# A two-block network on one core: a joined gated-delta mixer, with its adaptive row products behind the inversion

## The chip, the cores and the metric

The kernel runs on one core of one Trainium2 chip. The metric is the device time of one execution in microseconds (us). A core has TensorE (matrix products into PSUM banks), VectorE and ScalarE (elementwise work, the latter with functions such as the exponential), GpSimd (POOL) and SyncE (SP), which issues most loads. The profile calls TensorE's products PE and its weight loads PEld, VectorE DVE and ScalarE ACT.

## The reference, cut to what matters

Everything is fp32: a sequence of 256 tokens of width 1024 beside a context of 256 tokens. The first block is adaptive norm, a mixer, and a convolutional gated feed-forward net (FFN). Two further layers of other mixers and MLPs follow; the change hardly touches them.

```
mod = silu(c) @ w_ada + b_ada                    # shifts, scales and gates of the norms
q, k, v = silu(dwconv1d(h @ w_in, conv))         # 4 heads of 128; q and k then l2-normed
beta = sigmoid(ab); g = -exp(a_log) * softplus(ab + dt_bias)
gc    = cumsum(g in a chunk)
decay = where(lower, exp(gc[i] - gc[j]), 0)
a_mat = where(strict, (beta * k) @ k.T * decay, 0)
t_inv = inverse(eye + a_mat)                     # one per head, chunk, direction, sequence
for chunk: v_new = u - w @ S;  o = q_dec @ S + attn @ v_new;  S = S * exp(g_last) + k_dec.T @ v_new
y = concat(fourier(u), rmsnorm(o) * silu(z)) @ w_out
ffn: (silu(conv3x3(gate)) * val) @ w_down
```

The rule runs over the context first and then over the sequence, forward and backward.

## The kernel before, in words

Products in fp32 are mostly done in a split form: ScalarE copies a weight tile to a rounded high part (`whi`, L155) and VectorE subtracts it for the low part (`wlo`, L156). Three products then stand for one: high by high, high by low, low by high. Some products are plain fp32 (`cmn`, `tmn`). SP loads weights as tiles of 1 MB (`raw`, L161).

The mixer (`_block1_mix`, about 38 to 260 us) works on both sequences, s = 1 (context) and s = 0. For each it makes the gates (`gates1`, `gdn_scalars`, softplus and roots with few columns), projects and convolves k, turns it and multiplies it with itself (`kk`), and makes the decay masks (`decay`, L947: `gr - gc` plus the mask on VectorE, then one exponential). The scaled masks `Mall` (L785) hold 32 matrices of 128x128. `invert` turns their diagonal blocks of 32x32 with four transposes (L1029), solves all of them at once in 31 pairs of steps (L1039, L1041), and turns the results back (L1045). `merge` joins the 32-blocks on TensorE (y, z, zt), and `chain_step` runs the rule over four steps of chunks. Fourier products and gate products (`pu`) fill in between.

The adaptive rows (`ada_dot`) are a list of small pieces that `fill_step` issues at marked points: GpSimd's queue loads 512 KB into one of two tiles `nar` (L255), and one VectorE instruction (L259) takes its dot products. 10 of the first block's 24 stand before the inversion's end.

`project_out` (w_out) multiplies by its first half of channels, yields, and then by the second half, whose inputs come out of the rule. `begin` prepares the first two weight units of the FFN early and multiplies the first tokens (`part`, L496) as soon as they are normed. Engines run their instructions in the order in which a scheduler put them by priorities (`AHEAD`, `URGENT`) and dependences; a tile in a pool waits for the reader of the one whose place it takes. In the FFN each of 11 hidden tiles takes two weight units, a 3x3 convolution in 8 VectorE steps per half (L1290), and a product with w_down (L1274), two hidden tiles later.

Of the kernel before, what the change touches and what calls it, by code (L numbers as in the profile page):

```python
# [66 lines left out]
class Program:  # L67
# [67 lines left out]
    def softplus(self, out, in_, n):  # L135

        nc = self.nc
        T = lambda s: self.sm.tile([128, 16], F32, name=self.nm(s), tag=s, bufs=2)[:, :n]
# [25 lines left out]
    def units(self, src, count, nb, early=0):  # L164


        for u in range(count):
# [209 lines left out]
    def finish(self, banks, G, mod=None, between=None):  # L377
# [27 lines left out]
        with self.tc.high_priority(offset=URGENT):  # L405
            if mod is None:
                for t in range(2):
                    gain(t, 0)
                    gain(t, 1)
                    y[t][0](0)  # L410
                    y[t][0](1)
# [31 lines left out]

            gain(0, 0)
            gain(0, 1)
            y[0][0](0)
            y[0][0](1)
# [99 lines left out]
    def block1_mix(self):  # L547
        nc, tc = self.nc, self.tc
        self.yT = None
        with ExitStack() as ctx:  # L550
            self.work = self.pool(ctx, "work1", 2)
            self.nw1, self.ng2, self.nt2 = 6, 6, 1
# [72 lines left out]
    def conv_start(self, ps, i, out):  # L625

        nc = self.nc
        w = self.cwh
        x = self.W1("cvx")
# [3 lines left out]
        def rest():  # L633
            nc.vector.scalar_tensor_tensor(out=out[:, 1:], in0=x[:, :255], scalar=w[:, 3 * i:3 * i + 1], in1=out[:, 1:],
                                           op0=ALU.mult, op1=ALU.add)
            nc.vector.scalar_tensor_tensor(out=out[:, :255], in0=x[:, 1:], scalar=w[:, 3 * i + 2:3 * i + 3], in1=out[:, :255],
# [6 lines left out]
    def _block1_mix(self, g):  # L643
# [52 lines left out]
        pow_ = self.pow  # L696
        mods = next(mods)
        self.halves()
        del self.scratch
        for s in seqs:  # L700
            for k in range(8):
# [3 lines left out]
                else:  # L705
                    last = nc.vector.tensor_scalar(out=hT[s][k], in0=hT[s][k], scalar1=A[:, k:k + 1], scalar2=sh[:, k:k + 1], op0=ALU.mult, op1=ALU.add)
        wab = T([128, 8, 16], "wab", "wab")
        nc.sync.dma_start(wab, a["w_ab"])
        gates = {s: self.gates1(wab, hT[s], g, s) for s in seqs}
        for s in seqs:  # L710
            next(gates[s])

# [9 lines left out]
        def unit(u):  # L722
            return self.load(a["w_in"][u]).rearrange("p (k n) -> p k n", k=8)

        def split_unit(u, places):
            w = self.load(a["w_in"][u])
            with ExitStack() as ctx:
                if u >= 4:
                    ctx.enter_context(tc.issue_after(conv.ins))
                for i in range(2):  # L730
                    self.split(places[i], places[2 + i], w[:, i * 1024:(i + 1) * 1024])
# [7 lines left out]

        E, early = {}, deque((1, t, d) for t in range(2) for d in range(2))  # L740
        kT = {s: T([128, 4, 256], "kT", f"kT{s}") for s in seqs}
        kn = {s: T([128, 2, 4, 128], "kn", f"kn{s}") for s in seqs}
        ssq = {s: self.const.tile([128, 2, 4], F32, name=f"ssq{s}") for s in seqs}
        for u in range(2):
            w = split_unit(u, room("Zall") if u == 0 else room("atT0", "ut", "atT1", "sz"))
            for s in seqs:
                for m in range(2):
                    h = 2 * u + m
                    ps = self.PB("pk")
                    self.cm(ps, w, hp[s], m)  # L750
                    conv = self.conv_silu(ps, h, kT[s][:, h])
                    if (u, s, m) == (0, 1, 1):
                        self.hold = conv
                        gate = {s: next(gates[s]) for s in seqs}
                        scalars = {s: self.gdn_scalars(gate[s], ssq[s], g, s) for s in seqs}
                        gc = {s: next(scalars[s]) for s in seqs}
                    pt = self.pst.tile([128, 2, 128], F32, name=self.nm("tk"), tag="pst")
                    for t in range(2):
                        nc.tensor.transpose(pt[:, t], in_=kT[s][:, h, t * 128:(t + 1) * 128], identity=self.ident)
                    nc.scalar.activation(kn[s][:, :, h], pt, AF.Copy)  # L760
                    for t in range(2):
                        j = self.sm.tile([128, 128], F32, name=self.nm("j"), tag="j", bufs=2)
                        nc.scalar.activation(j, kn[s][:, t, h], AF.Square, accum_out=ssq[s][:, t, h:h + 1])
                    if u == 1 and early:
                        i = early.popleft()
                        E[i] = self.decay(gate[1][1], gc[1], i[2], i[1], None)
        sc = {s: next(scalars[s]) for s in seqs}
# [4 lines left out]
        Mall = T([128, 2, 2, 2, 4, 128], "Mall", "Mall")  # L772
        kd = {}
        for s in seqs:
            for t in range(2):
# [4 lines left out]
                for d in range(2):  # L780
                    if (s, t, d) not in E:
                        E[s, t, d] = self.decay(gate[s][1], gc[s], d, t, atT[t][:, d] if s == 0 else None)
                    e = E[s, t, d]
                    for h in range(4):
                        nc.vector.scalar_tensor_tensor(out=Mall[:, d, s, t, h], in0=kk[:, h], scalar=sc[s]["m"][:, d, t, h:h + 1],  # L785
                                                       in1=e[:, h], op0=ALU.mult, op1=ALU.mult)

        for s, ts in ((1, 0), (1, 1), (0, 0)):
            z = T([128, 2, 4, 128], "kd", "kd", bufs=3)
            for d in range(2):  # L790
                t = ts if s == 1 else d
                kd[d, s, t] = z[:, d]
                for h in range(4):
                    with tc.issue_after(roots.ins):
                        nc.gpsimd.tensor_scalar(out=z[:, d, h], in0=kn[s][:, t, h], scalar1=sc[s]["kd"][:, d, t, h:h + 1], scalar2=None, op0=ALU.mult)
# [1063 lines left out]
```

## Time and profile before

| | |
|---|---|
| median of 3 runs | 1671.67 us (1668.91 to 1674.85) |
| profiled execution | 1665.61 us, span 1663.8 us, granted clock 0.985 |
| PE busy | 1583.1 us (95%) |
| PEld busy | 1385.8 us (83%) |
| DVE busy | 1246.9 us (75%) |
| ACT busy | 866.7 us (52%) |
| POOL busy | 67.9 us (4%) |

The shares are means over stages with different limits. The mixer takes up to about 270 us, the first FFN about 300 to 505, the two layers the rest. A busy PE is not one at its peak: matmuls are pipelined, and the granted clock is a mean of two levels.

### The profile page before, as it was taken

The page shows a single profiled execution, that of the slowest core. Times are in us where ns is not written, and L with a number is a line of the kernel's source. Part 1 is how long each engine was busy: PE and PEld are TensorE (multiplying, and loading weights), DVE is VectorE, ACT ScalarE, POOL GpSimd, SP SyncE. Part 2 cuts the span into 40 slices and gives each one's busy share as a digit, 9 for nine tenths or more (in the row PEclk, how much of TensorE's full clock was granted, in tenths as well). Part 3 has the DMA queues.
Part 4 walks back from the last instruction along what each step waited for, and adds up shares of the span by engine and source line. Part 5 has one row for each costly group of instructions (what it writes and reads, how often), then busy time and mean ns, then how long its engine had stood idle before and what let it go on. Part 6 is the DMA issues. An engine that isn't in the chain of part 4 may idle for free.

```text
span 1663.8 us, 24724 instructions
## 1 busy us (share of the span) xinstructions
PE 1583.1 (95%) x9584; PEld 1385.8 (83%) x9584; DVE 1246.9 (75%) x2237; ACT 866.7 (52%) x1452; POOL 67.9 (4%) x103
## 2 busy tenths in 40 slices
PE   7969997999978999999999999999999999999998
PEld 2867986889967998888888899889988888879997
DVE  5898664899996794797768767777948877786554
ACT  4734453555445664655446544466646455564443
POOL 1150100000000000000000000000000000000000
PEclk9989999999988999999999999999999999999999
DMA  9332514456773554465665758746444656656552
GB/s 381 127 116 93 172 66 152 165 211 230 259 287 145 204 206 174 161 227 213 228 230 188 271 210 286 283 178 222 178 176 159 250 192 227 240 202 253 180 191 86
DMA packets 51669, 333.59 MB, mean 200 GB/s; under 512 B 6112, under 2 KB 6496, under 8 KB 14688
## 3 DMA queue, kind: packets, MB, share of 16 engines
q1 hardware_dynamic: 47808, 318.38, 52.5%
q0 software_dynamic: 3744, 13.63, 2.4%
q8 instruction: 75, 1.23, 0.3%
q14 instruction: 42, 0.34, 0.1%
HBM read 330.94 MB, written 1.05 MB: 200 GB/s over the span
## 4 chain that ended last, share of the span: by engine, by line
PE 75%; DVE 10%; ACT 5%; issue 5%; DMA 4%; POOL 1%; DVEq 0%; SPq 0%; POOLq 0%; ACTq 0%
PE pj L208 25%; PE pj L227 22%; PE bk L1274 11%; PE bk L227 4%; DVE wlo L156 2%; PE pj L496 2%; ACT whi L155 2%; DMA raw<-adaT 2%; PE pu L218 1%; DVE gac L1290 1%; DVE raw L259 1%; DMA raw<-w_down 1%; ACT xn L369 1%; DMA x<-x 1%; PE pk L208 1%
## 5 line engine op out<-in xcount | busy, mean ns | idle before, releaser
L156 DVE TENSOR_TENSOR wlo<-raw,whi 128x1024 fp32r<-128x1024 f32 x438 | 521.3, 1222 | 256.9 <-ACT whi L155 255.3
L155 ACT ACTIVATE whi<-raw 128x1024 fp32r<-128x1024 f32 x438 | 446.9, 1055 | 420.5 <-PE pj L208 177.4
L208 PE MATMUL pj<-hT,whi 128*128 128x256 f32 x2816 | 371.1, 284 | 5.5 <-ACT gac L1232 3.2
L208 PEld LDWEIGHTS pj<-hT,whi 128*128 128x128 f32 x2816 | 354.4, 192 | 10.6 <-ACT gac L1232 3.6
L1274 PE MATMUL bk<-whi,hid 128*128 128x512 f32 x688 | 187.7, 394 | 18.1 <-ACT hid L155 18.1
L208 PE MATMUL pj<-hT,wlo 128*128 128x256 f32 x1408 | 198.9, 284 | 0.0
L208 PEld LDWEIGHTS pj<-hT,wlo 128*128 128x128 f32 x1408 | 182.5, 193 | 0.4 <-issue 0.4
L227 PE MATMUL pj<-whi,hT 128*128 128x512 f32 x704 | 177.4, 394 | 0.6 <-ACT rgx L1693 0.6
L1274 PEld LDWEIGHTS bk<-whi,hid 128*128 128x128 f32 x688 | 127.3, 190 | 44.9 <-ACT hid L155 20.0
L227 PEld LDWEIGHTS pj<-whi,hT 128*128 128x128 f32 x704 | 130.9, 188 | 27.9 <-ACT rgx L1693 1.4
L259 DVE CUSTOM_DVE_ANT_0 raw<-raw,crow 128x1024 f32<-128x1024 f32 x104 | 124.9, 1221 | 10.5 <-DMA raw<-adaT 10.3
L1274 PE MATMUL bk<-wlo,hid 128*128 128x512 f32 x344 | 106.5, 391 | 0.0
L227 PE MATMUL pj<-wlo,hT 128*128 128x512 f32 x352 | 94.2, 389 | 0.0
L227 PEld LDWEIGHTS pj<-wlo,hT 128*128 128x128 f32 x352 | 66.1, 188 | 13.9
L1274 PEld LDWEIGHTS bk<-wlo,hid 128*128 128x128 f32 x344 | 65.0, 189 | 14.0
L1290 DVE SCALAR_TENSOR_TENSOR gac<-gin,cols,gac 128x189 f32<-128x189 f32 (+2 forms) x176 | 66.4, 430 | 1.8 <-ACT gac L1232 1.7
L496 PE MATMUL pj<-whi,hT 128*128 128x512 f32 x160 | 54.8, 413 | 2.0 <-POOL hT L441 1.1
L373 POOL TENSOR_TENSOR ss<-ss,nhalf 128x1 f32<-128x1 f32 x22 | 12.2, 554 | 811.2 <-DVE ss L372 811.2
L496 PEld LDWEIGHTS pj<-whi,hT 128*128 128x128 f32 x160 | 30.4, 194 | 12.1 <-ACT hT L432 2.9
L155 ACT ACTIVATE hid<-r 128x512 fp32r<-128x512 f32 x32 | 20.2, 630 | 36.5 <-DVE r L1326 36.4
L259 DVE CUSTOM_DVE_ANT_0 nar<-nar,crow 128x1024 f32<-128x1024 f32 x24 | 29.3, 1222 | 8.9 <-DMA nar<-adaT 8.8
L432 ACT ACTIVATE hT<-tp,sh,A 128x128 fp32r<-128x128 f32 x80 | 30.2, 460 | 10.9 <-PE tp L425 7.5
(429 smaller groups left out, 2200.3 us busy)
## 6 DMA issues: line engine op xcount, KB each, us to landing
raw<-w_in SPq DMA_DIRECT2D x98, 1024.0 KB, 4.9
raw<-mlp_w SPq DMA_DIRECT2D x64, 1024.0 KB, 4.9
raw<-adaT SPq DMA_DIRECT2D x52, 1024.0 KB, 4.9
raw<-w_up SPq DMA_DIRECT2D x22, 1024.0 KB, 4.9
nar<-adaT POOLq DMA_DIRECT2D x24, 512.0 KB, 4.3
raw<-w_out SPq DMA_DIRECT2D x12, 1024.0 KB, 4.8
raw<-w_down SPq DMA_DIRECT2D x11, 1024.0 KB, 5.0
raw<-lru_w_o SPq DMA_DIRECT2D x8, 1024.0 KB, 4.8
```

The lines of the kernel that those rows point to most:

```text
L155: self.nc.scalar.activation(hi, v, AF.Copy)
L156: self.nc.vector.tensor_tensor(out=lo, in0=v, in1=hi.bitcast(F32), op=ALU.subtract)
L208: self.nc.tensor.matmul(ps, lhsT=ww[k][:, m * 128:(m + 1) * 128], rhs=xx[k], start=(i == 0 and k == 0), stop=(i == 2 and k == 7))
L218: self.nc.tensor.matmul(ps, lhsT=x[k][:, t * 128:(t + 1) * 128], rhs=w[:, k, :], start=(k == 0), stop=(k == 7))
L227: self.last_product = self.nc.tensor.matmul(ps, lhsT=xx[k0 + k][:, t * 128:(t + 1) * 128], rhs=ww[k], start=(k0 == 0 and i == 0 and k == 0 ...
L259: nc.vector.tensor_tensor_reduce(out=r, in0=r, in1=self.crow[vec], scale=0.5, scalar=0.0, op0=ALU.mult, op1=ALU.add, accum_out=out[:, k:k ...
L369: self.queue("a", lambda: nc.scalar.activation(junk[:, i * 512:(i + 1) * 512], parts[i], AF.Square, scale=1.0 / 32, accum_out=ss[:, i:i + 1]))
L373: self.queue("g", lambda: nc.gpsimd.tensor_tensor(out=ss[:, 3:4], in0=ss[:, 2:3], in1=self.nhalf, op=ALU.pow))
L432: q("a", lambda: nc.scalar.activation(H[0][k][:, tk(t)], ps[t, g][:, j], AF.Identity, scale=A[:, k:k + 1], bias=sh[:, k:k + 1]))
L496: self.nc.tensor.matmul(self.early[t], lhsT=H[lo][k][:, tk], rhs=ww[k % 4], start=(lo == j == i == 0), stop=(lo == 1 and j == 7))
L1274: self.last_product = self.nc.tensor.matmul(banks[t][h], lhsT=xx[:, k, t * 128:(t + 1) * 128], rhs=ww[k][:, h * 512:(h + 1) * 512], start= ...
L1290: self.nc.vector.scalar_tensor_tensor(out=acc[:, r, c], in0=gin[:, ri, ci], scalar=w, in1=acc[:, r, c], op0=ALU.mult, op1=ALU.add)
```

## The change

1. Gates and scalars are made for both sequences in one set, with softplus over 32 columns and one root over 16. Sums of decays are turned into rows (`gcrows`), in a high and a low part. `decay` spreads a row on TensorE: a product that puts the mask into the bank, and four that add the row; ScalarE's exponential takes the other sum as its bias. The scale of v moves into kd and into `ro`, so that `chain_step` copies v plainly.
2. k and v of both sequences are convolved in pairs, 512 columns in a tile. The first unit of k is plain fp32.
3. ScalarE copies the diagonal blocks into `invD`, with 128 rows, so that one transpose goes each way; eight copies put the result into `Zall`.
4. `fill_step` is no longer called among v's convolutions. It is called in the chain, where it now waits for the inversion, the roots and the copies, and once in each gate unit. q's convolutions are finished behind the first merge.
5. Four units of w_out take places that are free in the mixer; the last of the four is loaded into the pool `more`.
6. w_down's units are loaded straight into `whi` and `wlo` places as two halves of 512 KB, and the products are plain fp32 with an unsplit hidden tile.
7. `finish` squares before it multiplies by the gain; in the MLPs the hidden tiles from 14 on have a high priority.

The core of the diff:

```
     for h in range(4):
-        nc.tensor.matmul(gr[:, h], lhsT=gg[:, d, t, h:h + 1].to_broadcast([128, 128]),
-                         rhs=self.U if d == 0 else self.L, start=True, stop=True)
...
+            nc.tensor.matmul(gr, lhsT=self.mask[:, 0], rhs=self.mask[:, mask:mask + 1].to_broadcast([128, 4, 128]), start=True, stop=False)
             for h in range(4):
-                nc.vector.scalar_tensor_tensor(out=e[:, h], in0=gr[:, h], scalar=gc[:, d, t, h:h + 1], in1=mask,
-                                               op0=ALU.subtract, op1=ALU.add if sign > 0 else ALU.subtract)
-            nc.scalar.activation(e, e, AF.Exp, scale=float(sign))
+                i = 16 * d + 4 * h + 2 * s + t
+                nc.tensor.matmul(gr[:, h], lhsT=self.choose[:, i:i + 1].to_broadcast([64, 128]), rhs=self.gcrows, start=False, stop=h == 3)
+            for h in range(4):
+                nc.scalar.activation(e[:, h], gr[:, h], AF.Exp, scale=float(sign), bias=gc[sign][:, d, h, s, t:t + 1])
...
+                for b in range(4):
+                    q = slice(32 * b, 32 * b + 32)
+                    nc.scalar.activation(D[q, :, s, t], Mall[q, :, s, t, :, q], AF.Copy)
...
-        for b in range(4):
-            q = slice(32 * b, 32 * b + 32)
-            nc.vector.transpose(B[q].rearrange("m j i -> m i j"), Mf[q, :, q].rearrange("j m i -> j i m"))
+        nc.vector.transpose(B.rearrange("m j i -> m i j"), Df.rearrange("j m i -> j i m"))
...
+                    for s in seqs:
+                        self.cmn(ps[:, s], w, hT[s], m)
...
-                    if m == 0:
-                        with tc.issue_after(last.ins), tc.issue_after(pow_.ins), tc.issue_after(self.hold.ins):
-                            self.fill_step()
...
-                with tc.issue_after(self.turned_back.ins):
+                with tc.issue_after(self.turned_back.ins), tc.issue_after(roots.ins), tc.issue_after(self.z_copied.ins):
                     self.fill_step()
...
-        self.wout = self.project_out("w_out", yT, EARLY)
+        self.wout = self.project_out("w_out", yT, 4)
...
+            if plain:
+                with self.tc.high_priority(offset=AHEAD):
+                    tiles = [self.hl.tile([128, 1024], F32R, name=self.nm(tag), tag=tag, bufs=self.nhl).bitcast(F32) for tag in ("whi", "wlo")]
+                    for h, z in enumerate(tiles):
+                        self.nc.sync.dma_start(z, src(u)[:, h * 1024:(h + 1) * 1024])
+                yield Weights(tiles, nb(u)), None
+                continue
...
-        p = [(whi, hid[:, 0]), (whi, hid[:, 1]), (wlo, hid[:, 0])]
+        p = [(whi, hid[:, 0]), (whi, hid[:, 1]), (wlo, hid[:, 0])] if wlo else [(whi, hid)]
```

VectorE's row before, at the start of the inversion (`invB` the turned blocks, `nar` with `gc` an adaptive dot, `qT` and `vT` convolutions):

```order
L636 SCALAR_TENSOR_TENSOR qT_1038<-cvx_1138,cwh,qT_1038 128x255
L1029 STREAM_TRANSPOSE invB<-Mall_906 32x32x32 x4
L259 ISA nar_1452,gc_1265<-nar_1452,crow_1266 128x1024
L259 ISA gc_1265 128x1
L1039 TENSOR_TENSOR invt<-invB,invX 128x31
L634 SCALAR_TENSOR_TENSOR vT_1277<-cvx_1278,cwh,vT_1277 128x255
L1041 TENSOR_TENSOR invX<-invX,invt 128x31
L639 SCALAR_TENSOR_TENSOR qT_1038<-cvx_1138,qT_1038 128x256
```

and the same place now:

```order
L645 SCALAR_TENSOR_TENSOR qT_897<-cvx_962,cwh,qT_897 128x255
L1069 STREAM_TRANSPOSE invB<-invD_739 128x32x32
L648 SCALAR_TENSOR_TENSOR qT_897<-cvx_934,qT_897 128x256
L648 SCALAR_TENSOR_TENSOR qT_897<-cvx_962,qT_897 128x256
L1079 TENSOR_TENSOR invt_1035<-invB,invX 128x31
L643 SCALAR_TENSOR_TENSOR qT_897<-cvx_997,cwh,qT_897 128x255
L1081 TENSOR_TENSOR invX<-invX,invt_1035 128x31
L643 SCALAR_TENSOR_TENSOR qT_897<-cvx_1025,cwh,qT_897 128x255
```

One transpose over 128 rows stands for four over 32, and no adaptive dot is left there; the first one now stands in VectorE's row among the merge's and the chain's steps (`Zall`, `zc` parts of the merge, `pqs` and `qs` of q's root):

```order
L246 SCALAR_TENSOR_TENSOR crow_1424<-nar_1426,crow_1424 128x1024
L648 SCALAR_TENSOR_TENSOR vT_1249<-cvx_1250,vT_1249 128x512
L1198 TENSOR_SCALAR Zall<-z_1299 32x4x32 x2
L267 ISA nar_1429,gc_1423<-nar_1429,crow_1424 128x1024
L267 ISA gc_1423 128x1
L1198 TENSOR_SCALAR zc_1282<-z_1313 32x4x32 x2
L267 ISA nar_1430,gc_1423<-nar_1430,crow_1424 128x1024
L267 ISA gc_1423 128x1
L1198 TENSOR_SCALAR Zall<-z_1341 64x4x64
```

All 24 dots follow in this manner, one or two between the steps.

ScalarE's row before, at the end of the mixer (`raw_2567` and `raw_2577` the FFN's first two units, `raw_2499` and `raw_2509` the second half of w_out, `yv` the rule's outputs):

```order
L155 ACTIVATE whi_2569<-raw_2567 128x1024
L155 ACTIVATE whi_2573<-raw_2567 128x1024
L155 ACTIVATE yT_2367<-yv_2459 128x256
L155 ACTIVATE yT_2367<-yv_2466 128x256
L155 ACTIVATE yT_2367<-yv_2473 128x256
L155 ACTIVATE whi_2579<-raw_2577 128x1024
L155 ACTIVATE whi_2583<-raw_2577 128x1024
L155 ACTIVATE yT_2367<-yv_2480 128x256
L155 ACTIVATE whi_2501<-raw_2499 128x1024
L155 ACTIVATE whi_2505<-raw_2499 128x1024
L155 ACTIVATE whi_2511<-raw_2509 128x1024
```

and now (`raw_2299` and `raw_2309` the second half of w_out, `raw_2367` the FFN's first unit):

```order
L155 ACTIVATE whi_2301<-raw_2299 128x1024
L155 ACTIVATE whi_2305<-raw_2299 128x1024
L155 ACTIVATE yT_2163<-yv_2259 128x256
L155 ACTIVATE yT_2163<-yv_2266 128x256
L155 ACTIVATE yT_2163<-yv_2273 128x256
L155 ACTIVATE whi_2311<-raw_2309 128x1024
L155 ACTIVATE whi_2315<-raw_2309 128x1024
L155 ACTIVATE yT_2163<-yv_2280 128x256
L377 ACTIVATE xn_2389,ss_2391<-bk_2182 128x512
L377 ACTIVATE xn_2389,ss_2391<-bk_2183 128x512
L155 ACTIVATE whi_2369<-raw_2367 128x1024
```

The second half of w_out is split ahead of the FFN's units. The load of `raw_2309` into the pool `more`, whose place lies over tiles of the mixer, waits for the last product of the first half.

## Rows read from the trace of the kernel before

**Rows 1.** Totals of the page: busy us (share), instructions.

```profile
PE 1583.1 (95%) x9584; PEld 1385.8 (83%) x9584; DVE 1246.9 (75%) x2237; ACT 866.7 (52%) x1452; POOL 67.9 (4%) x103
```

**Rows 2.** Windows: busy us of PE, PEld, DVE, ACT, POOL; clock; DMA share; GB/s.

```profile
38.00:163.00 125.00, 106.67 (x666) 92.60 (x666) 115.74 (x339) 64.22 (x179) 30.07 (x40) 0.95 0.34 118
121.00:163.00 42.00, 37.54 (x182) 30.78 (x182) 39.70 (x108) 21.02 (x63) 2.32 (x2) 0.96 0.26 89
163.00:270.00 107.00, 105.90 (x770) 93.00 (x770) 57.38 (x153) 43.43 (x124) 8.93 (x15) 1.00 0.35 119
270.00:307.30 37.30, 27.18 (x121) 21.19 (x122) 30.12 (x54) 25.13 (x50) 3.51 (x5) 0.91 0.37 131
345.00:487.00 142.00, 142.00 (x984) 133.22 (x983) 137.97 (x245) 74.12 (x98) 0.00 (x0) 0.99 0.67 246
487.00:508.00 21.00, 7.98 (x25) 5.89 (x24) 14.26 (x26) 5.77 (x11) 0.56 (x1) 0.67 0.50 175
```

**Rows 3.** Chain of waits, 70 to 125 us: start, length, what.

```profile
78.01 2.58 POOL rs L133
...
100.00 4.54 DVE wk L156 x4
...
110.06 2.09 DVE invB L1029
...
120.71 39.69 issue
```

**Rows 4.** Groups on DVE, 38 to 163 us: count; busy us, mean ns; idle before.

```profile
L259 DVE CUSTOM_DVE_ANT_0 nar<-nar,crow 128x1024 f32<-128x1024 f32 x10 | 12.2, 1222 | 0.0
L1041 DVE TENSOR_TENSOR invX<-invX,invt 128x31 f32<-128x31 f32 (+15 forms) x31 | 10.5, 339 | 0.4
...
L1029 DVE STREAM_TRANSPOSE invB<-Mall 32x1024 f32<-32x1024 f32 x4 | 8.6, 2150 | 0.0
L947 DVE SCALAR_TENSOR_TENSOR E<-gr,gc,cst 128x128 f32<-128x128 f32 x24 | 7.2, 342 | 0.3 <-PE gr L942 0.3
...
L947 DVE SCALAR_TENSOR_TENSOR atT<-gr,gc,cst 128x128 f32<-128x128 f32 x16 | 4.5, 341 | 0.0
L634 DVE SCALAR_TENSOR_TENSOR kT<-cvx,cwh,kT 128x255 f32<-128x255 f32 x8 | 3.9, 482 | 0.6 <-ACT kT L631 0.6
```

**Rows 5.** Chain of waits, 163 to 310 us.

```profile
246.36 13.81 PE pu L218 x64
...
269.63 4.76 DMA raw<-w_up
274.50 1.07 ACT whi L155
...
279.57 12.58 PE bk L227 x48
```

**Rows 6.** What PE waited for: us in total, times, longest.

```profile
PE bk L1274 <- ACT hid L155: 18.1, 5, 12.7
PE bk L227 <- ACT whi L155: 8.4, 1, 8.4
```

**Rows 7.** Products of 512 columns: two rows of the chain, one of PE's timeline.

```profile
233.94 1.73 PE f L1163 x4
...
355.62 5.47 PE bk L1274 x24
...
221.56 1.98 PE L1163 MATMUL f<-dft,ut 128*128 128x512 f32 x4
```

**Rows 8.** Adaptive dots: landing of their loads, waits for them, first and last issue.

```profile
  DVE nar L259: 8.8, 6
...
DMA to landing us min/median/max: 3.9/4.4/13.1
...
162.07 0.69 POOL L255 DMA_DIRECT2D nar<-adaT  x1
...
206.83 0.53 POOL L255 DMA_DIRECT2D nar<-adaT  x1 [2.83 <-DVE A L259]
```

More of the change, by code (lines that the diff above doesn't have):

```diff
@@ L162, in load, with units @@
         return r
-    def units(self, src, count, nb, early=0):
+    def units(self, src, count, nb, early=0, plain=False):
         for u in range(count):
@@ L407, in finish @@
                 for t in range(2):
[L408 to L411, printed above, removed]
+                    for h in range(2):
+                        y[t][0](h)
+                        gain(t, h)
                     y[t][1]()
@@ L720, in _block1_mix @@
         hp = {s: (Blocks(parts[s][:2]), Blocks(parts[s][2:])) for s in seqs}
-        def unit(u):
-            return self.load(a["w_in"][u]).rearrange("p (k n) -> p k n", k=8)
         def split_unit(u, places):
             w = self.load(a["w_in"][u])
[L727 to L731, printed above, removed]
+            for i in range(2):
+                self.split(places[i], places[2 + i], w[:, i * 1024:(i + 1) * 1024])
             return Weights(places[:2], 256), Weights(places[2:], 256)
@@ L738, in room, with unit @@
             return [T([128, 1024], "wk", t, F32R) for t in tags]
+        def unit(u):
+            return self.load(a["w_in"][u]).rearrange("p (k n) -> p k n", k=8)
         E, early = {}, deque((1, t, d) for t in range(2) for d in range(2))
-        kT = {s: T([128, 4, 256], "kT", f"kT{s}") for s in seqs}
-        kn = {s: T([128, 2, 4, 128], "kn", f"kn{s}") for s in seqs}
-        ssq = {s: self.const.tile([128, 2, 4], F32, name=f"ssq{s}") for s in seqs}
-        for u in range(2):
[L745 to L757, printed above, removed]
@@ new lines, in _block1_mix @@
+        kTs = T([128, 2, 4, 256], "kT", "kT")
+        kT = [kTs[:, s] for s in range(2)]
+        kns = T([128, 2, 2, 4, 128], "kn", "kn")
+        kn = [kns[:, s] for s in range(2)]
+        ssq = self.const.tile([128, 4, 2, 2], F32, name="ssq")
+        for u in range(2):
+            w = split_unit(u, room("Zall")) if u else unit(u)
+            for m in range(2):
+                h = 2 * u + m
+                ps = self.PB("pk", (128, 2, 256))
+                for s in seqs:
+                    if u:
+                        self.cm(ps[:, s], w, hp[s], m)
+                    else:
+                        self.cmn(ps[:, s], w, hT[s], m)
+                self.conv_silu(ps, h, kTs[:, :, h])
+                if h == 0:
+                    gate = next(gates)
+                    scalars = self.gdn_scalars(gate, ssq, g)
+                    gc = next(scalars)
+                pt = self.pst.tile([128, 2, 2, 128], F32, name=self.nm("tk"), tag="pst")
+                for s in seqs:
@@ L764, in _block1_mix @@
[L764 to L767, printed above, removed]
+                        nc.scalar.activation(j, kn[s][:, t, h], AF.Square, accum_out=ssq[:, h, s, t:t + 1])
+                if u == 1:
+                    for i in (early.popleft(), early.popleft()):
+                        E[i] = self.decay(gc, 1, i[2], i[1], None)
+        sc = next(scalars)
@@ new lines, in gates1 @@
+        ab = {}
+        for s in (1, 0):
+            ps = (self.pst if s else self.psd).tile([16, 256], F32, name=self.nm("ab"), tag="pst" if s else "psd")
+            for k in range(8):
+                nc.tensor.matmul(ps, lhsT=wab[:, k, :], rhs=hT[s][k], start=(k == 0), stop=(k == 7))
+            ab[s] = self.work.tile([16, 256], F32, name=self.nm("abs"), tag="w1", bufs=self.nw1)
+            nc.scalar.activation(ab[s], ps, AF.Copy)
+        yield
+        ps = self.pst.tile([128, 2, 2, 16], F32, name="abt", tag="pst")
@@ new lines, in gates1 @@
+        for s in (1, 0):
+            for t in range(2):
+                nc.tensor.transpose(ps[:, s, t], in_=ab[s][:, t * 128:(t + 1) * 128], identity=self.ident[0:16, 0:16])
+        pc = ps.rearrange("p s t c -> p c (s t)")
+        beta = g.tile([128, 2, 4, 2, 2], F32, name="beta")
+        gg = g.tile([128, 2, 4, 2, 2], F32, name="gg")
+        by = lambda z: z.rearrange("p d h s t -> p (d h) (s t)")
+        fl = lambda z: z.rearrange("p d h s t -> p (d h s t)")
+        xx = self.sm.tile([128, 8, 4], F32, name="xx", tag="xx", bufs=1)
```

274 lines of the change are left out of this document (148 added, 126 removed).

## The prediction

> **What bounds the kernel now.** I read the page's totals first. TensorE is busy 95% of the span [rows 1], so a stage gains only where it idles or loses matmuls. The windows show where that is: from 38 to 163 us, where the decay masks and the 32x32 inversions are made, it has 106.7 of 125 us, 18.3 us idle, while VectorE has 115.7; from 163 to 270, the chain over the chunks, TensorE has 105.9 of 107; from 270 to 307.3 it idles 10.1; from 345 to 487 it is full, VectorE having 138; the end of the first FFN (487 to 508) has 8 us of matmuls in 21 at a granted clock of 0.67, a mean of its two levels (1.2 and 2.4 GHz) after VectorE's splits left TensorE idle [rows 2]. After 508 the change hardly moves an instruction.
>
> The chain of waits says what holds the first stretch: the root on GpSimd, the scaled masks on VectorE, then block transposes and 39.7 us of "issue", short steps with no named wait [rows 3]. VectorE's groups give the durations [rows 4]. The chain from 246 to 292 and the list of TensorE's waits give the next two places [rows 5, 6]. The span is 1663.8 us and the profiled execution 1665.61; the median of the runs shown, 1671.67, is 6.1 us above it. Differences are worked out in the profile and put on the median.
>
> **Up to the inversion's end.** VectorE's work in 38 to 163 falls by parts:
> - The adaptive dots leave: 10 x 1.222 = 12.2 [rows 4], and one row of weights made once, about as long as one: 13.4 us.
> - The block transposes: 8 of 2.15 us on 32 partitions [rows 4] become 2 on all 128 with the same 1024 elements per partition: 17.2 to 4.3, 12.9 us less. If duration went with all elements, each would take 8.6 and nothing would be saved; I take the lower end, since all rows of VectorE here go by the elements per partition: 0.34 us for 128, 1.22 for 1024, on 128 partitions.
> - L947's 40 additions go: 7.2 + 4.5 = 11.7 us [rows 4]. TensorE spreads the rows instead: for each of 10 masks a 128x512 product (0.228 us by 5.47/24 [rows 7]) and four of 128 columns, against 32 fp32 products of 128 columns (7 us at 0.22, half of the 256-column pitch below). At 0.06 us per narrow product, a quarter of 0.228, it is 4.7 us, 2.3 less; at fp32's 0.22 it is 11.1, 4.1 more. I take 0, between them: this stretch has idle TensorE time for either.
> - Convolutions of pairs: 8 fewer groups of three calls save the fixed part of 24 calls. From 0.48 us at 255 columns and 0.34 at 128 [rows 4] 0.20 of a call is fixed: 5 us. The query convolution (12 calls, about 5 us) moves behind, and two splits of 1.22 go, 2.4 us.
>
> Together 13.4 + 12.9 + 11.7 + 5 + 5 + 2.4 = 50 of VectorE's 116 us leave. Against that stand 16 copies of the diagonal blocks and 6 of the 8 copies back on ScalarE, which has 64 of 125 us busy [rows 2], and the first key unit in plain fp32: 32 products of 256 columns at 0.432 (13.81 us for 32, two records each) [rows 5] for 96 of the split form at 0.114 (half of 0.228), 13.8 for 10.9, so 2.9 us more. One root over 16 columns replaces two of 8, the longer of which took 2.58 us on the chain [rows 3]: between 2.6 and 5.2. The merge of the blocks starts at 163 now. VectorE alone would be done at 163 - 50 = 113, but the scaled masks wait for both key units and the root as now and end near 102 (now at 100, ahead of four splits [rows 3]); then come the block copies and one transpose (5), the inversion's steps (31 pairs, 10.5 us for each half [rows 4], 21), the query convolutions between them (5), and the transpose and copies back (4): 102 + 35 = 137. By the time removed it could be as early as 128, by waits for GpSimd's memsets as late as 145.
>
> **Up to the first half of the output projection (269.5).** Matmuls are not removed, so the idle time is all there is to win: 18.3 + 1.1 = 19.4 us [rows 2]. In the new order the 24 dots stand behind the inversion. Their weights come through GpSimd's queue into two buffers, and 14 issues from 162.07 to 206.83 us make 3.4 us per dot, landing 4.4 us after issue [rows 8]; 24 of them take 83 us, in VectorE's order among the chain's own steps, where 14 now take 45. Each chain step that stands behind a dot whose weights are under way waits. VectorE waits 8.8 us in all for these weights now [rows 8], and TensorE was full beside it because Fourier and the gate products fill in. I take 6 us of idle time left (0 to 20): minus 13.4.
>
> The Trainium skill, SBUF — State Buffer, section "SBUF: two separate sides", says that a VectorE copy that uses both its ports locks GpSimd out and so delays transfers issued from GpSimd. Here half of the transfers landed within 4.4 us, the shortest in 3.9 and the longest in 13.1 [rows 8], beside a VectorE that is 54 to 93% busy [rows 2], so the trace shows it at most in a few. By the rule in full, each of the 10 dots added to the chain would be later by a copy, about 0.4 us by VectorE's rows, 4 us in all, and this term minus 9.4.
>
> **To the early FFN products (307.3).** Now ScalarE splits the first FFN unit ahead of the second half of the output projection, and TensorE waits 8.4 us there [rows 6]; the chain shows load 4.76, splits to 279.57, 12.58 us of products [rows 5]. In the new order the third unit of the output projection is split at once, but the fourth is loaded only when the first half's products are done: 4.8 us of load and two splits of 1.06 and 1.22 each [rows 4, 5], about 9.5 us less the 6.3 us of products that the third unit covers (half of 12.58). The wait falls from 8.4 to 4, 4 us less; if the load starts late, 3 more.
>
> **First FFN.** 88 products of 128x512 in plain fp32 replace 264 at 0.228: 0.684 becomes 0.865 (1.73 us for two, four records) [rows 7], 88 x 0.181 = +15.9 us on TensorE, full from 345 to 487. 22 splits and 11 hidden splits leave VectorE, 22 x 1.222 + 11 x 0.69 = 34 us, so that it has slack. What this wins is the end: 13.0 idle and some 2.3 of slow clock in 487 to 508 [rows 2]; the chain has VectorE's last splits there, and the longest wait for the last hidden tile is 12.7 [rows 6]. With plain weights the last two pairs of products, 13.8 us, cover the last tile's additions. Net 0 (minus 5 to plus 13, when the end stays as it is). The order of square and gain at each end is worth 0; smaller waits after 508 minus 1 (0 to minus 2).
>
> Sum: minus 13.4, minus 4, 0, minus 1: minus 18. 1671.7 - 18 = 1654.
>
> **Rivals.**
> *TensorE is the bound and gives the gain back.* VectorE's 50 us leave, but the matmuls of values and gates, which now fill the inversion (37.5 of 42 us [rows 2]), are then done later, at the chain. For it speaks the full stretch 163 to 270, against it the 18.3 us idle. Only a quarter of the idle time goes: minus 5, minus 4 at the projection, plus 4 in the FFN: 1667.
> *The dots set the chain.* If it ends 34 us after the last issue, as now (206.8 and, where the gate products start, 241), it ends at 137 + 24 x 3.4 + 34 = 253 and the first half of the products at 281: plus 12, minus 4, minus 1: 1679. With the four dots that stand in the gate units taken out it ends at 239, minus 2 - 4 - 1: 1665. I take the middle, 1672. For it speak 3.4 us per dot; against it, that two buffers allow 3.1 (4.4 + 0.5 + 1.2 for two dots), and that TensorE is full beside them now.
> *Slower: fp32 in the FFN costs more than the row says.* The row is from two products in a row. Where the array has to start anew each may take 0.99 us (another such pair took 1.98 us [rows 7]): 88 x 0.306 = 27 us, and the end's 13 us stay, since the last tile's chain of additions sets it: 27 - 18 = +9: 1681. It decides from 0.945 us per product, (18 + 5)/88 above 0.684. Against it: 32 products with new weights each go at 0.432 for half the columns, exactly half [rows 5].
> *All idle time goes.* Everything from 38 to 270 fills, 19.4, the second half has no wait, 8, the FFN gains 5: 1639.
>
> **Chances.** Forecast 0.59 (1644 to 1664 by its own bounds), TensorE full 0.12, dots 0.12, slower 0.09, all idle 0.08. A difference within 0.3%, 5 us, can't be told from none. The rival at 1667 lies on that line and counts half as faster; that at 1672 counts as the same but for 0.02 slower and 0.03 faster: faster 0.59 + 0.08 + 0.06 + 0.03 = 0.76, same 0.06 + 0.07 = 0.13, slower 0.11. The range goes from 1638, the last rival, to 1671, past the one at 1667 and half of the dots', and leaves out the slower one.
>
> **What would show it.** Right: the merge starts by 140; TensorE idles under 8 us from 38 on until the first half of the output products ends, at 253 to 259; 24 dots at 3.1 to 3.4 us; the FFN's end has under 4 us idle at full clock, its products 0.865 us each; TensorE's full time after 508 the same. Wrong: a chain that ends at 240 with waits for the dots' weights; products above 0.9 us; transposes of more than 3 us; or the wait for the fourth unit above 8 us.

## The result, and the profile after

The changed kernel takes 1649.03 us (median of 4 runs, 1648.7 to 1652.61) against 1673.26 (1668.91 to 1675.81): a ratio of 0.9863 (0.9836 to 0.9889), 24.2 us. Its profiled execution took 1648.7 us with a span of 1646.9, so the two traces differ by 16.9 us of span. The rest, about 7 us, is that the profiled execution of before, 1665.61, was 7.7 us faster than its median; a second profile of it (below) shows where.

Totals of the page of after [rows 1], busy us, share of the span and instructions:

```profile
PE 1598.1 (97%) x9445; PEld 1363.5 (83%) x9445; DVE 1190.0 (72%) x2101; ACT 840.4 (51%) x1415; POOL 69.9 (4%) x102
```

The same stretches as in [rows 2], of after; the columns are length, busy us of PE, PEld, DVE, ACT and POOL, then clock, DMA share and GB/s:

```profile
38.00:163.00 125.00, 116.49 (x713) 98.92 (x713) 85.01 (x226) 77.97 (x211) 27.99 (x36) 0.99 0.28 99
...
345.00:487.00 142.00, 142.00 (x839) 109.70 (x838) 114.47 (x219) 50.00 (x72) 0.00 (x0) 1.00 0.69 247
487.00:508.00 21.00, 20.39 (x71) 11.54 (x70) 13.27 (x30) 12.51 (x31) 3.50 (x5) 1.00 0.21 76
```

VectorE lost 31 us up to 163, and the FFN's end is full at full clock. Fixed times no longer hold the same work, though, so the accounts go from landmark to landmark. First before: to the merge's start, to the end of the first half of w_out, to the last early FFN product, to the first w_down product, to 505, to the first layer's early products, to the end.

```profile
38.00:160.30 122.30, 104.23 (x648) 90.54 (x649) 113.48 (x333) 63.39 (x177) 27.75 (x38) 0.94 0.34 121
38.00:269.50 231.50, 212.14 (x1434) 185.41 (x1435) 172.87 (x490) 107.24 (x301) 39.00 (x55) 0.97 0.34 119
269.50:308.20 38.70, 28.51 (x129) 22.11 (x128) 31.27 (x55) 25.54 (x50) 3.51 (x5) 0.91 0.38 135
308.20:342.40 34.20, 28.80 (x218) 27.26 (x216) 31.18 (x57) 17.13 (x26) 0.00 (x0) 1.00 0.61 214
342.40:505.00 162.60, 149.85 (x1013) 139.81 (x1014) 153.29 (x272) 79.43 (x106) 0.00 (x0) 0.95 0.67 243
505.00:520.60 15.60, 12.05 (x52) 9.34 (x51) 11.40 (x25) 10.87 (x27) 3.50 (x5) 0.89 0.12 35
520.60:1663.80 1143.20, 1122.75 (x6644) 992.81 (x6644) 828.99 (x1293) 611.93 (x909) 17.25 (x25) 1.00 0.58 209
```

The same work in after:

```profile
38.00:140.10 102.10, 94.08 (x540) 78.74 (x539) 74.00 (x206) 62.42 (x175) 23.19 (x31) 0.98 0.25 87
38.00:262.40 224.40, 212.22 (x1379) 181.42 (x1379) 147.83 (x387) 110.51 (x292) 41.15 (x57) 0.99 0.36 124
262.40:303.60 41.20, 31.18 (x123) 23.55 (x121) 32.47 (x56) 25.37 (x50) 5.31 (x5) 0.88 0.39 139
303.60:335.10 31.50, 30.78 (x217) 26.60 (x215) 27.42 (x54) 13.62 (x22) 0.00 (x0) 1.00 0.65 233
335.10:497.90 162.80, 162.79 (x944) 124.16 (x944) 128.00 (x249) 56.27 (x85) 1.11 (x2) 1.00 0.67 240
497.90:506.80 8.90, 8.32 (x41) 5.99 (x40) 7.81 (x19) 8.20 (x19) 2.40 (x3) 1.00 0.17 59
506.80:1646.90 1140.10, 1122.30 (x6644) 992.01 (x6644) 828.37 (x1293) 611.36 (x909) 17.26 (x25) 1.00 0.58 210
```

The mixer to the first half of w_out: 231.5 to 224.4, 7.1 less, all of it idle time (19.4 to 12.2). The second half and early FFN products: 2.5 more. The FFN (three rows): 212.4 to 203.2, 9.2 less: its idle time fell from 21.7 to 1.3, its busy time rose from 190.7 to 201.9. The rest: 3.1 less, 2.6 of it in the first layer. Together 16.9.

The chain of waits of after, 38 to 310 and 330 to 500 [rows 3, 5, 7] (start, length, what):

```profile
86.52 2.92 POOL rs L133
...
136.54 2.10 DVE invD L1082
...
251.51 10.92 PE bk L235 x48
...
346.88 6.87 PE bk L1321 x16
...
477.31 20.62 PE bk L1321 x48
```

VectorE's groups of after up to the merge [rows 4], one of k's convolutions in pairs and the transposes: count, busy us, mean ns, idle before.

```profile
L643 DVE SCALAR_TENSOR_TENSOR kT<-cvx,cwh,kT 128x510 f32<-128x510 f32 x4 | 3.0, 747 | 6.5 <-ACT kT L640 6.5
...
L1069 DVE STREAM_TRANSPOSE invB<-invD 128x1024 f32<-128x1024 f32 x1 | 2.3, 2275 | 0.5 <-ACT invD L800 0.5
...
L1082 DVE STREAM_TRANSPOSE invD<-invX 128x1024 f32<-128x1024 f32 x1 | 2.1, 2093 | 0.0
```

One transpose takes as long on 128 rows as on 32; the last ends at 138.64, and the merge begins at 140.10 (before, 160.30). A plain product takes 0.859 us (16 records are 8 products). What TensorE waited for in after [rows 6], us in total, times, longest:

```profile
PE tp L432 <- DVE xn L411: 7.7, 4, 3.6
...
PE pj L503 <- DVE wlo L156: 3.6, 2, 2.9
...
PE bk L235 <- ACT yT L155: 2.3, 2, 1.5
...
PE bk L1321 <- ACT hid L155: 2.0, 3, 0.8
```

The 12.7 for the last hidden tile and the 8.4 for w_out's split are gone. The dots of after [rows 8], 140 to 245: shortest, median and longest in ns, first and last start; who waited; landing.

```profile
L267 DVE CUSTOM_DVE_ANT_0 nar<-nar,crow x24: 1206/1224/1226, 149.3 to 237.1; 128x1024 f32<-128x1024 f32 x24
...
  DVE nar L267: 10.6, 7
...
DMA to landing us min/median/max: 3.9/4.3/7.5
```

From the first of the 24 dots to the last it is 87.8 us, 3.8 for each of the 23 steps. VectorE waits 10.6 us for them; TensorE idles 3.4 of the 97 us from 145 to 242.

### The profile page after: what moved, and what is told of

Its sections match the earlier page's. It is cut to its first block, busy times and chain, and to the rows that moved or that the text cites. A ratio compares the mean times of both kernels' runs of the same rounds, so it can differ in the third digit from the quotient of the medians.

```text
span 1646.9 us, 24238 instructions
## 1 busy us (share of the span) xinstructions
PE 1598.1 (97%) x9445; PEld 1363.5 (83%) x9445; DVE 1190.0 (72%) x2101; ACT 840.4 (51%) x1415; POOL 69.9 (4%) x102
## 4 chain that ended last, share of the span: by engine, by line
PE 76%; DVE 8%; DMA 5%; ACT 5%; issue 3%; POOL 2%; DVEq 0%; POOLq 0%; SPq 0%; ACTq 0%
PE pj L216 26%; PE pj L235 22%; PE bk L1321 13%; PE bk L235 3%; PE pj L503 2%; ACT whi L155 2%; DVE wlo L156 1%; DMA raw<-adaT 1%; DMA raw<-w_in 1%; PE pk L222 1%; POOL kd L809 1%; DVE raw L267 1%; DMA nar<-adaT 1%; DMA x<-x 1%; DVE invX L1081 1%
## 5 line engine op out<-in xcount | busy, mean ns | idle before, releaser
L156 DVE TENSOR_TENSOR wlo<-raw,whi 128x1024 fp32r<-128x1024 f32 x416 | 493.9, 1221 | 275.2 <-ACT whi L155 273.7
L155 ACT ACTIVATE whi<-raw 128x1024 fp32r<-128x1024 f32 x416 | 422.5, 1054 | 409.8 <-PE pj L216 195.8
L216 PEld LDWEIGHTS pj<-hT,whi 128*128 128x128 f32 x2816 | 353.3, 192 | 10.6 <-ACT fq L1661 3.0
L1321 PE MATMUL bk<-whi,hid 128*128 128x512 f32 x600 | 183.4, 421 | 2.0 <-ACT hid L155 2.0
L1321 PEld LDWEIGHTS bk<-whi,hid 128*128 128x128 f32 x600 | 110.1, 188 | 38.4 <-issue 16.3
L1321 PE MATMUL bk<-wlo,hid 128*128 128x512 f32 x344 | 123.8, 441 | 0.0
L235 PE MATMUL pj<-wlo,hT 128*128 128x512 f32 x352 | 94.2, 389 | 0.0
L267 DVE CUSTOM_DVE_ANT_0 nar<-nar,crow 128x1024 f32<-128x1024 f32 x24 | 29.2, 1219 | 10.7 <-DMA nar<-adaT 10.6
L503 PE MATMUL pj<-wlo,hT 128*128 128x512 f32 x80 | 33.1, 413 | 3.6 <-DVE wlo L156 3.6
```

What stands on the lines that cost most here:

```text
L155: self.nc.scalar.activation(hi, v, AF.Copy)
L156: self.nc.vector.tensor_tensor(out=lo, in0=v, in1=hi.bitcast(F32), op=ALU.subtract)
L216: self.nc.tensor.matmul(ps, lhsT=ww[k][:, m * 128:(m + 1) * 128], rhs=xx[k], start=(i == 0 and k == 0), stop=(i == 2 and k == 7))
L235: self.last_product = self.nc.tensor.matmul(ps, lhsT=xx[k0 + k][:, t * 128:(t + 1) * 128], rhs=ww[k], start=(k0 == 0 and i == 0 and k == 0 ...
L267: nc.vector.tensor_tensor_reduce(out=r, in0=r, in1=self.crow[vec], scale=0.5, scalar=0.0, op0=ALU.mult, op1=ALU.add, accum_out=out[:, k:k ...
L503: self.nc.tensor.matmul(self.early[t], lhsT=H[lo][k][:, tk], rhs=ww[k % 4], start=(lo == j == i == 0), stop=(lo == 1 and j == 7))
```

## The experiments

Each edits the changed kernel, unless it says before. Medians are beside those of before on the same chip, with the 95% interval of the ratio.

**The FFN: the split w_down put back, and the plain one alone.**

```
-            banks = self.feed(hidden, "w_down", 11, 2, True)
+            banks = self.feed(hidden, "w_down", 11, 2)
...                                                        # and the hidden tile split again
```

> The changed kernel with w_down in the split form again (three fp32r products, hidden tile split by ScalarE and VectorE). Theory A: plain w_down is worth what the trace shows between the first full FFN products and the next layer's early products, 212 us before and 203 now, so this run is about 9 us slower than the changed kernel, 1658 us, with TensorE waiting 10 us or more for the last hidden tile. Rival B: plain fp32 only costs (88 products at 0.865 for 264 at 0.228, 15.9 us on a full TensorE) and the FFN's shorter end comes from the order of square and gain: then this run is faster, about 1640 to 1645 us.

1660.97 against 1672.8, 0.9937 (0.9918 to 0.9956): 12 us given back. Then part 6 alone, put into before:

```
-            banks = self.feed(hidden, "w_down", 11, 2)
+            banks = self.feed(hidden, "w_down", 11, 2, True)
...                                                        # units straight into whi, wlo; hid unsplit
```

> The kernel before with plain w_down alone. Theory A: it brings the same 9 us here, 1673 to about 1664, and the wait for the last hidden tile (12.7 us) is gone. Rival B: 16 us on a full TensorE less the 13 idle at the end, 1673 to 1676. Rival C: what the kernel before loses in its ordinary runs above its profiled one (1673 against 1666) also lies in this end, and the gain is 15 us, 1658.

1660.08, 0.9928 (0.9908 to 0.9948): 12.7 less than before. Plain w_down is worth half of the whole by either road. TensorE's timeline at the FFN's end (start, us, engine, line, what, idle time ahead), first before:

```profile
499.91 2.08 PE L1274 MATMUL bk<-whi,hid 128*128 128x512 f32 x4 [12.74 <-ACT hid L155]
501.79 1.05 PE L1274 MATMUL bk<-wlo,hid 128*128 128x512 f32 x2
...
506.20 1.07 PE L1274 MATMUL bk<-whi,hid 128*128 128x512 f32 x4
...
511.20 1.08 PE L425 MATMUL tp<-cst,xn 128*128 128x128 f32 x4 [3.48 <-DVE xn L403]
```

with w_down split again in the changed kernel:

```profile
496.98 2.08 PE L1321 MATMUL bk<-whi,hid 128*128 128x512 f32 x4 [12.14 <-ACT hid L155]
...
503.46 1.07 PE L1321 MATMUL bk<-whi,hid 128*128 128x512 f32 x4
...
508.22 1.17 PE L432 MATMUL tp<-cst,xn 128*128 128x128 f32 x6 [3.24 <-DVE xn L411]
```

and the changed kernel:

```profile
496.89 1.02 PE L1321 MATMUL bk<-wlo,hid 128*128 128x512 f32 x2
498.01 1.09 PE L432 MATMUL tp<-cst,xn 128*128 128x128 f32 x8
```

The wait of 12 us, the products at half clock behind it (2.08 for four records, 1.07 to 1.1 later) and the wait for the next norm come back with the split and go without it. The last is a gain that no step of the forecast had: without the wait the last two hidden tiles' products run in a row, all those of the first tokens first, and ScalarE reads the first finished sums at 489.37 while TensorE multiplies until 498. With the wait, the last tile's products for all tokens come together behind it.

**Only some of w_down's units plain**: those from 7 on, and 2, 5, 8, 9, 10.

```
+PLAIN = lambda u: u >= 7            # second kernel: u in (2, 5, 8, 9, 10)
...                                  # units and hidden tiles plain or split by it
```

> The changed kernel with only the last four of the 11 w_down units plain, the first seven split again (hidden tiles likewise). Theory A: what plain w_down brings is the end of the FFN, and its price is 1.45 us of TensorE per unit in a stretch that TensorE fills: seven units less give up to 10 us back, while VectorE's 155 us of the FFN's 194 rise by 22 to 177 and still fit: 1639 to 1644. Rival B: VectorE becomes the bound in the middle, as in the kernel before, and TensorE waits there for what it saves: 1649 to 1655. Rival C: the end's wait comes back: 1655 or more.

> The changed kernel with units 2, 5, 8, 9 and 10 of w_down plain and six split. Theory A of the run with the last four: 6 x 1.45 = 8.7 us back at most, 1640 to 1645, and if VectorE falls behind over seven split units in a row, this even mixture does better than the other. Rival B: no better than all plain, 1649.

1650.19 (0.9877, 0.9851 to 0.9903) and 1649.72 (0.987, 0.9845 to 0.9896): by the medians as the changed kernel. From 335 to 480 VectorE is then busy for 140.25 and 136.94 us of 145, in after for 117.95. The two traces do show a shorter FFN: from its first full product to the second set of the next layer's norm products it is 202.2 us in after (303.45 to 505.68), and 4.7 and 3.0 less here, half or less of the 10 and 8.7 that theory A had. TensorE waits 3.2 and 3.6 us at its start for the convolution's sums (0.7 in after). Behind the FFN these executions took 1.8 and 4.3 us more than that of after. The first has the fastest run of all, 1642.86, but its six go up to 1655.07, so nothing is shown to be faster, and why the medians don't show what the FFN won stays open.

**The inversion made longer**: each transpose as four, over 32 rows.

```
-        nc.vector.transpose(B.rearrange("m j i -> m i j"), Df.rearrange("j m i -> j i m"))
+        for b in range(4):
+            q = slice(32 * b, 32 * b + 32)
+            nc.vector.transpose(B[q].rearrange("m j i -> m i j"), Df[q].rearrange("j m i -> j i m"))
```

> The changed kernel with each of the inversion's two transposes done as four of 32 partitions again, 6 more of 2.1 us: 12.9 us more ahead of the merge and no matmul more. Theory A: TensorE has other matmuls to draw forward; as the merge came 18.4 us earlier by the change and the first w_out products ended 7.1 us earlier, 0.4 us per us, this run is about 5 us slower, 1654. Rival B: the inversion sets the end by its whole length: 1662. Rival C: TensorE is the bound and the inversion is hidden: 1649.

1660.78, 0.994 (0.9922 to 0.9958): 11.8 more than the changed kernel. VectorE's transposes there, and this run's windows: all to the end of the first half of w_out, and 145 to 160 around the merge's start at 152.84.

```profile
L1071 DVE STREAM_TRANSPOSE invB<-invD 32x1024 f32<-32x1024 f32 x4 | 8.6, 2160 | 2.4 <-ACT invD L800 2.3
...
L1086 DVE STREAM_TRANSPOSE invD<-invX 32x1024 f32<-32x1024 f32 x4 | 8.1, 2024 | 0.1
```

```profile
38.00:273.10 235.10, 218.45 (x1379) 187.69 (x1380) 160.20 (x393) 110.80 (x292) 41.32 (x57) 0.96 0.34 119
...
145.00:160.00 15.00, 10.35 (x52) 9.38 (x51) 11.92 (x12) 9.35 (x21) 1.07 (x2) 0.77 0.37 134
```

The stretch ahead of the transposes, here and then in after:

```profile
79.00:100.00 21.00, 18.59 (x105) 15.58 (x104) 13.76 (x50) 15.65 (x52) 12.59 (x18) 0.84 0.21 75
...
79.00:100.00 21.00, 18.00 (x113) 15.04 (x114) 13.56 (x49) 15.97 (x53) 12.75 (x18) 0.96 0.23 76
```

12.3 us more of transposes bring the merge 12.7 later and the first half's end 10.7: 4.5 of it is idle time, and 6.2 is more busy time for the same 1379 matmuls, at a clock of 0.96 for 0.99. Not all of that clock is the edit's. From 79 to 100, before the first transpose starts at 102.44, it was 0.84 for 0.96, some 2.5 us by estimate (21 us times 0.12); from 145 to 160, behind the wait, 0.77 for 1.00, some 3.5. So waiting costs twice here, by the wait and by the clock behind it, and about 8 of the 10.7 us are shown to be the edit's in this execution.

**The inversion made shorter**: the second 15 of its 31 pairs of steps left out, so that part of the inverses isn't computed.

```
-        for i in range(31, 0, -1):
+        for i in range(31, 15, -1):
```

> The changed kernel that leaves out the second 15 of the inversion's 31 pairs of steps on VectorE (30 instructions, about 10.5 us); their part of the inverses is not computed, everything behind runs as before. Adding 12.9 us there cost 11.8. Theory A: in the other direction the price falls off, since TensorE has only 12.2 us of idle time left from 38 us to the end of the first w_out products, 7 us of it before the merge: 3 to 5 us faster than the changed kernel, 1644 to 1646. Rival B: the same price both ways, 0.9 us per us: 1639 to 1640. Rival C: TensorE is the bound already: 1648 to 1649.

1647.1, 0.9861 (0.9837 to 0.9886): 2 us less, inside the runs' spread (1646.13 to 1653.8). VectorE turns the result back at 122.36, 14.2 us sooner, but the merge starts at 138.70, 1.4 sooner: TensorE's row has v's products in front of it until then. So the change has brought VectorE's inversion down to where TensorE's own row ends: longer costs 0.7 to 1.0 us for each (8 by the trace and 11.8 by the medians, for 12.3), shorter gains little. The profiled execution, 1652.24, is one of the two long ones of the six; the other four lie between 1646.13 and 1647.97, 1 to 3 us below the changed kernel. Its windows show a clock loss of another kind, and TensorE's timeline the waits ahead of it:

```profile
140.00:150.00 10.00, 7.28 (x55) 6.53 (x53) 4.72 (x10) 4.84 (x11) 1.08 (x2) 0.98 0.61 216
150.00:160.00 10.00, 9.81 (x45) 8.12 (x45) 3.93 (x8) 5.11 (x17) 1.08 (x2) 0.51 0.44 143
160.00:170.00 10.00, 9.56 (x83) 8.95 (x84) 3.67 (x9) 4.25 (x8) 2.96 (x3) 1.00 0.22 75
```

```profile
143.50 1.16 PE L1173 MATMUL y<-Zall,Mall 128*128 128x128 f32 x8 [1.10 <-ACT Zall L1168]
...
150.19 1.11 PE L1173 MATMUL y<-zT,Mall 128*64 128x64 f32 x8 [1.81 <-ACT zT L1201]
```

**The dots put back in front**: `fill_step` called again among v's convolutions, so that 8 dots stand in the inversion.

```
+                with tc.issue_after(roots.ins):
+                    self.fill_step()
```

> The changed kernel with eight of the 24 adaptive dots and the row of weights issued from v's convolutions, so that they stand among the inversion's steps. Theory A: the inversion ends 11 us later (9 instructions of 1.22 us), at 0.4 us per us 4 to 5 us, less what VectorE no longer waits for dots in the chain (TensorE idles only 3.4 of 97 us there): 1651 to 1653. Rival B: the dots cost as much in the chain as in the inversion: 1649.

1655.57, 0.9912 (0.9897 to 0.9927): 6.5 more. The result is turned back at 157.49 instead of 136.54, and TensorE waits for v. TensorE's window to the first half of w_out, its longest wait there, and VectorE's:

```profile
38.00:269.80 231.80, 216.43 (x1379) 186.55 (x1380) 146.73 (x388) 109.88 (x292) 39.49 (x57) 0.96 0.34 121
```

```profile
PE tv L841 <- DVE vT L648: 8.9, 1, 8.9
```

```profile
112.55 1.23 DVE L246 SCALAR_TENSOR_TENSOR crow<-nar,crow 128x1024 f32<-128x1024 f32 x1 [7.00 <-ACT nar L245]
```

TensorE idles 15.4 us in this window (12.2 in after). Of the 21 us, 11 are the nine instructions and 9.9 are VectorE's waits, 7.0 of them for the row of weights, whose load starts only at 105.0, and 2.9 for weights of dots. The kernel before made that row at 54.60, without a wait. So this is not the order of before, and the 6.5 us are the price of the dots and of that wait together; what the dots alone cost in front is not shown.

**w_out: the early units, and the fourth's place.**

```
-        self.wout = self.project_out("w_out", yT, 4)
+        self.wout = self.project_out("w_out", yT, EARLY)
```

> The changed kernel with only the first two w_out units in the mixer's free places. Theory A: from the end of the first half of the w_out products to the first full FFN products the changed kernel needs 41.2 us, the kernel before 38.7; the load of the fourth unit into the pool of the second FFN unit holds that unit up. This run takes 38 to 39 there and is 2 to 3 us faster, 1646 to 1647. Rival B, the step as predicted: four units are worth 4 us, and this run is at 1653.

```
-                r = self.load(src(u), self.more if u == early - 1 else None)
+                r = self.load(src(u), self.more if u == early - 1 == EARLY - 1 else None)
```

> The changed kernel with the fourth w_out unit loaded into the ordinary load tiles, ahead of the FFN's units, and the separate pool left to the FFN's second unit. Theory A: the wait for that unit's low part (3.6 us of TensorE) goes, and the second half of the products starts earlier: 41.2 us from the first half's end to the FFN's full products become 36 to 37, 1644 to 1645. Rival B: the splits of the fourth unit now stand ahead of the rule's outputs in ScalarE's row and hold up what was won: 1649.

1650.76 (0.9873, 0.9851 to 0.9895) and 1650.16 (0.9874, 0.9856 to 0.9891): neither can be told from the changed kernel. With two early units the old wait is back:

```profile
PE bk L235 <- ACT whi L155: 8.4, 1, 8.4
```

and the whole stretch still takes 39.5 us, where the changed kernel takes 41.2. TensorE's timeline of the changed kernel shows what ate the gain:

```profile
283.46 1.97 PE L432 MATMUL tp<-cst,xn 128*128 128x128 f32 x8 [3.56 <-DVE xn L411]
...
290.92 0.50 PE L503 MATMUL pj<-wlo,hT 128*128 128x512 f32 x1 [2.93 <-DVE wlo L156]
```

The second half is done 17.5 us after the first (before, 22.8), but then TensorE waits for the norm of the tokens and for the low part of the second FFN unit, which is loaded behind w_out's fourth. With the fourth in `raw` the latter wait falls to 1.5; the one for `yT` is then 2.7 (2.3 in two pieces in after), ScalarE's splits of that unit standing ahead of `yT`, and the stretch takes 39.6.

**The two small parts**: the finish order undone, and the MLPs' priority taken away.

```
-                    for h in range(2):
-                        y[t][0](h)
-                        gain(t, h)
+                    gain(t, 0)
+                    gain(t, 1)
+                    y[t][0](0)
+                    y[t][0](1)
...                                  # and the same where a layer begins
```

> The changed kernel with gain before square again at the ends. Theory A: the handover from the first FFN to the next layer fell from 15.6 to 8.9 us since the first token half's banks are done 10 us before the last product, not by the order: within 2 us of the changed kernel, 1649 to 1651. Rival B: the order makes the 6.7 us: 1656.

```
-                    if i >= 14:
+                    if i >= 99:
```

> The changed kernel with the MLPs' last hidden tiles at their ordinary priority. Theory A: the 2.7 us that layer 0's MLP end gained come from this: 1651.5 to 1652. Rival B: they come with the earlier start of the layers (other loads): 1649.

1649.47 (0.9866, 0.9845 to 0.9887), nothing; and 1653.23 (0.9894, 0.9876 to 0.9912), 4.2 more, though its runs (1649.55 to 1655.68) overlap those of the changed kernel. Without the priority TensorE waits 2.6 and 3.2 us at the end of the first layer's MLP where it now waits 0.5 and 2.6, and the first layer is 4.4 us longer; the second is the same. But the run with five plain units has the priority, waits 4.3 us at that place and has a first layer 4.2 us longer. So what the priority is worth can't be told from the scatter.

**Before, profiled again.** Nothing is edited.

> The kernel before, unchanged, profiled once more: its profiled execution took 1665.6 us and its other runs 1667 to 1677. Theory A: the difference lies in the first FFN, where TensorE waits for VectorE's splits at the start and at the end: from 308 us to the next layer's early products it takes more than the 212 us of the first profile, the mixer the same. Rival B: it lies in the mixer's chain of the inversion, or evenly over the layers.

This execution took 1672.01 us, 6.4 more than the first one profiled. 3.9 us are lost by the FFN's start: from 38 to 160 its granted clock was 0.92 instead of 0.94. 1.0 is lost in the FFN and 1.5 behind it. So about 6 of the 24 us stand in the choice of execution, and between these two executions most of it lies ahead of the FFN, at a lower clock.

## Why the prediction was right, and where it was wrong

1654 was forecast from 1671.7, and 1649 came: faster, and inside the range. The parts were not right one by one: up to the FFN the change gave 12.8 us less than forecast, in the FFN and the layers 11.3 more. That the sum fits so well is luck; that it is faster is not. Of the forecast's own signs, the merge's start and the full end of the FFN came true, while the idle time up to w_out's first half (12.2 for under 8), its end (262.4 for 253 to 259) and the pace of the dots did not.

- *Up to the inversion's end: right in the time, not in every part.* The merge was put at 137 (128 to 145) and starts at 140.10. The transposes took 4.4 us (4.3 forecast), a convolution of a pair 0.747 us against twice 0.482, the root 2.92. VectorE's work ahead of the merge fell by 39.5 us, not 50. Two parts of the 50 failed: only 8 of the 10 dots stood ahead of the merge, and q's convolutions, 5 us, did not move behind it. All 12 of their calls run from 98.7 to 109.6, between the masks and the inversion's first steps (before, 105.6 to 124.2), although the code finishes them behind the first merge: the scheduler's order decides. The longer inversion shows that time saved here was on the path.
- *Minus 13.4 up to the first half of w_out: mechanism right, size wrong; minus 7.1.* The failed step is "I take 6 us of idle time left": 12.2 is left, 8.0 of it ahead of the merge and 4.2 behind. That VectorE is done sooner doesn't fill TensorE, whose row of v's products ends at the same time, as the shorter inversion shows. By this trace the rival in which TensorE is the bound, with minus 5 here, was the nearer one; against the second profile of before, where the first half ends at 271.9, the gain is 9.5.
- *The dots: the order right, the pace off.* 3.8 us each, not 3.1 to 3.4. As feared, VectorE waits behind them, but TensorE only 3.4 us. So the rival with the dots on the chain fell. Moved back in front they cost 6.5, with the wait for their row of weights. The Trainium skill, SBUF — State Buffer, section "SBUF: two separate sides", has GpSimd-issued transfers held up by VectorE's two-port copies. The 13.1 us of [rows 8], which the prediction took for such a transfer, is one of SP's loads into `nar` at the start (9.6 to 13.1). From 160 to 245 the transfers issued from GpSimd landed in 3.9 to 5.7 us before, median 4.3, and from 140 to 245 in 3.9 to 7.5 after, median 4.3. So the median shows no hold-up; a delay of 0.4 us in some of them can be neither seen nor excluded.
- *Minus 4 to the early FFN products: wrong, plus 2.5.* "The wait falls from 8.4 to 4, 4 us less" is the step (its own 9.5 less 6.3 leaves 3.2). The wait fell further, to 1.5 and less; the gain was lost one step on, at the norm and the second FFN unit. With two early units the time is the same, so part 5 is worth nothing that can be measured.
- *FFN net 0: wrong, minus 9.2.* The cost was right: 88 products at 0.859 instead of 0.684 are 15.4 us (15.9 forecast), and the rival with slower fp32 fell. What was mis-sized is the gain, 13 idle and 2.3 of clock: idle time fell by 20.4, since the start and the handover to the first layer were counted at nothing, and busy time rose by 11.2 only, so by difference some 4.2 came back from the clock, 0.95 and 0.89 in the last two rows before and 1.00 after. With w_down split again the wait at the FFN's start is back (4.0 us), so this gain too is plain w_down's.
- *Finish order 0: right. After 508 minus 1: minus 3.1*, most of it in the first layer. It is no more than what this stretch differs by among executions, so that the priority made it is not shown.

Open: why executions of one kernel scatter by 6 to 12 us. The traces show stretches at a lower clock, whose place changes (from 79 to 100 us the granted clock lies between 0.84 and 1.00 in kernels that do the same work there); what places them was not found. The parts undone add up to more than the whole; that those in the mixer overlap is likely, not shown. The gates in one set, the masks made on TensorE and the convolutions in pairs were not tried by themselves.

## What to carry to other kernels

Before counting an engine's shorter work as a gain, ask which row the other engine still has in front of it at that place: 12.3 us more cost 12 on one side of the balance, 14.2 less gained 2 on the other. A wait at a stage's end is priced with what comes behind it, the slow clock and the next stage's start, which here made the cheaper-looking split dearer by 12 us. Where two waits follow each other on different inputs, ending the first only shows the second.

## What the hardware showed that was not expected

- A plain fp32 product of 512 columns took 0.859 us, 3.77 times a split one's 0.228: three split products save 0.175 us of TensorE and cost VectorE and ScalarE their splits.
- A block transpose with 1024 columns took 2275 ns on 128 rows and 2160 on 32, as the forecast had assumed: its time went with the columns, not with all elements.
- Idle times of 1.10 and 1.81 us within 143 to 150 were followed by 10 us at a granted clock of 0.51, the level of 1.2 GHz, with TensorE 98% busy; then it was 1.00. A wait of 12.7 us was followed by products at half rate for some 5 us.
